# Second-half convolution taps issued among the attention's steps, and a thinner stream of modulation rows, in a two-layer mixer block

## The chip, the core and the metric

The program runs on one core of one Trainium2 chip. Its measure is device time in microseconds (us), the median of several executions. The core has five engines with their own instruction streams: TensorE (PE; its weight loads are shown apart, as PEld), VectorE (DVE), ScalarE (ACT), GpSimd (POOL) and SyncE (SP). Here PE does the matrix products, DVE and ACT the elementwise work, SP issues the loads of weight chunks, and POOL issues the loads of modulation rows.

## The reference, cut to what matters

A first block of two layers (`DEPTH = 2`), then a second block that the change doesn't touch. A layer of the first block is a mixer over 256 tokens x of width 1024 and 256 context tokens; layer 0 computes outputs for both (512 columns), layer 1 for x alone (256 columns).

```
for l in range(2):
    shift, scale, gate = split(silu(c) @ w_mod[l] + b_mod[l])      # for c and c_ctx
    h = rmsnorm(x, norm_w[l]) * (1 + scale) + shift
    p = h @ w_in[l]                                                # all branches' inputs
    r = head_norm(retention(p)) * silu(ret_z)
    s = b * conv3(c * xv) * silu(sc_z)
    f = silu(layer_norm(conv31(a * sigmoid(g)) + bias)) * silu(cf_z)
    a = windowed_attention(rope(q), rope(k), v, ctx) * silu(att_z)
    merged = sum(sigmoid(gate_i) * (branch_i @ w_branch[i]))       # r, s, f, a
    x = x + gate * (merged @ w_out[l])
# second block: its own modulation, 6 rows of columns per layer
mod = silu(c_2) @ ada_w[i] + ada_b[i]
```

`conv31` is a depthwise convolution with 31 taps over four tiles of 128 channels. Its layer norm needs all four tiles.

## The kernel before, in words

Everything is kept with channels on the partitions and tokens in the columns. Each matrix product of weights is in three parts (high and low halves in fp32r): `mm3` issues three matmuls, `tile_gemm` 24 of them for one tile of 128 outputs. A weight chunk of 512 KB is loaded by SP (`wr`), ACT makes its high half (`wh`), DVE its low half (`wl`, L169). Four chunks are held at a time. The planner of the language orders each engine's instructions: the earlier one is issued in the program, the earlier it comes, as far as its inputs are there in the planner's own clock.

The side work of a mixer (convolution, attention, layer norm, retention) stands in generators in the queue `hiq`. Each `yield` names the cost of a step in us. After every product tile the kernel calls `pump(bud)` (`proj` with `bud`, `gates` with 1.5 `bud` for each of its 8 tiles), which adds credit and issues steps from the front of `hiq` until the credit is used up. A second queue, `loq`, holds the modulation rows of the coming parts: 8 rows for layer 0's gate and 24 for layer 1 (`wmodT`), then 96 for the second block (`adaT`). One row is a 512 KB load issued by POOL (L485) into one of two buffers of the tag `ad`, and a DVE pass over it (`junk`, L495), two passes where both c and c_ctx need it. `loq` gets `ratio` times the pumped us, from the 11th pump of layer 0 and the 31st of layer 1 on.

```
self.credit = min(self.credit + us, 8.0)
while self.credit > 0 and self.hiq:
    ...
        self.credit -= next(self.hiq[0])
...
if self.pumps > 0:
    self.spare = min(self.spare + self.ratio * us, 4.0)
while self.spare > 0 and self.loq:
    c, fn = self.loq.popleft()
    self.spare -= c
    fn()
```

A row with two passes costs 2.3, with one 1.15. A pass may not come before the instruction that was issued ten marked DVE instructions earlier (`with self.tc.issue_after(self.marks[0])`; `marks` holds the last ten `tt` and `stt` instructions). `until(st, key)` issues steps from the front of `hiq`, whatever the credit, until the part named by `key` is done. `flush_lo(mark)` does the same for `loq`: at the end of layer 0 until layer 1's rows are done, at the end of layer 1 until the second block's 96 rows are done. After the latter, `ada_columns` makes `afw` from them, and each tile of the output projection of layer 1 is turned into an input of the second block with `afw` (`raw_tile`: an ACT and a DVE instruction `r<-x,afw`), for the 96 matmuls of 258 columns that follow.

The order of a mixer in product tiles: (layer 0: four tiles for the convolution's input, pumped), four query tiles, one k and one v tile; then 16 tiles of the short convolution; gates(1) (8 tiles, each 36 matmuls); `until att`; four z tiles for the attention's output; gates(3); eight q and k tiles of the retention and its v tiles (pumped 8 times with a quarter of `bud`, twice that in layer 0); `until ln`, after which `ratio` is 0.6; four z tiles, gates(2), four z tiles, gates(0); then the 8 tiles of the output projection, each pumped with 0.5.

Convolution: `conv(0)` does the taps for channel tiles 0 and 1, `conv(2)` those for tiles 2 and 3, in 31 steps each; a step is two DVE instructions (L183, `t<-t,cfw,t`). Attention: `att_prep` and the rope steps, then four `att_pair`s; 84 steps with a cost of 37.4 in layer 0, 68 steps with 25.4 in layer 1. The layer norm's steps cost 11.3 and 5.9.

Of the kernel before, what the change touches and what calls it, by code (L numbers as in the profile page):

```python
# [2 lines left out]

# [1 line left out]

# [99 lines left out]
class Core:  # L105
# [110 lines left out]
    @staticmethod  # L216
    def pipe(gens, depth):

        wait, live = deque(gens), []
        while wait or live:  # L220
            if wait and len(live) < depth:
                live.append(wait.popleft())
            for g in list(live):
                try:
                    yield next(g)
                except StopIteration:
                    live.remove(g)


    def feed(self, *src):  # L230
# [648 lines left out]
    def mixer(self, l, hs, N, first, mod, norm):  # L879
        nc, A = self.nc, self.A  # L880
        NS = N // S
        bud = (3.0, 1.0)[l]
        self.pumps, self.spare = -(10, 30)[l], 0.0
        self.ratio = (0.5, 0.6)[l]
        if l:
            self.src.extend(self.mixer_chunks(l))
        self.ahead()
# [27 lines left out]
        def conv(i):  # L915

            for j in (i, i + 1):
                us[j] = self.T(N)
                c = l * 124 + 15 * 4 + j
                self.ts(us[j], glu[j], self.cfw[:, c:c + 1], ALU.mult, self.par("cf_conv_b", l * 4 + j), ALU.add)  # L920
            yield 0.6 * NS
            for k in range(31):
                if k == 15:
                    continue
                d = k - 15
                lo, hi = max(0, -d), min(S, S - d)
                for j in (i, i + 1):
                    c = l * 124 + k * 4 + j
                    u = v3(us[j])[:, :, lo:hi]
                    self.stt(u, v3(glu[j])[:, :, lo + d:hi + d], self.cfw[:, c:c + 1], u, ALU.mult, ALU.add)  # L930
                yield 0.6 * NS
            if i == 2:
                glu.clear()
# [7 lines left out]
        def layer_norm():  # L941
            sm = self.T(N)
            self.tt(sm, us[0], us[1], ALU.add)
            self.tt(sm, sm, us[2], ALU.add)
            self.tt(sm, sm, us[3], ALU.add)
            yield 1.0 * NS
            mb = self.psa()[:, :N]
            self.mmul(mb, self.inv[512].to_broadcast([P, P]), sm)
            yield 0.1
            sq = self.T(N)  # L950
            for i in range(4):
                self.tt(us[i], us[i], mb, ALU.subtract)
                if i == 0:
                    self.act(sm, us[i], AF.Square)
                else:
                    self.act(sq, us[i], AF.Square)
                    self.tt(sm, sm, sq, ALU.add)
            yield 1.3 * NS
            rows = self.psa()[0:1, :N]
            self.row_sum(rows, 0, 1, [sm], 512, True, True)  # L960
            yield 0.1
            cols = self.columns(rows, 1, N)
            r = self.small(2 * NS)
            self.rsqrt(r, cols[:, :, 0])
            yield 0.2
            rb = self.psa()
            for t in range(2 * NS):
                self.spread(rb[:, t * P:(t + 1) * P], r[:, t:t + 1])
            yield 0.1
            for i in range(4):  # L970
                self.stt(us[i], us[i], self.par("cf_ln_w", l * 4 + i), rb[:, :N], ALU.mult, ALU.mult)
            yield 1.3 * NS
            for i in range(4):
                t = self.T(N)
                self.act(t, us[i], AF.Tanh, scale=0.5, bias=lnb2[:, i:i + 1])
                self.ts(us[i], us[i], self.par("cf_ln_b", l * 4 + i), ALU.add)
                self.stt(us[i], t, 1.0, us[i], ALU.add, ALU.mult)
                yield 0.45 * NS
            st["ln"] = 1
# [43 lines left out]
            self.hiq.append(rest())  # L1023
            self.hiq.append(conv(0))
        self.hiq.append(conv(2))
        self.hiq.append(layer_norm())


        rot, cs = const(C_ROT, 384), const(C_COS, 512)
# [28 lines left out]
        def att_prep():  # L1058
            yield from rope(kraw)
            for g in range(2):  # L1060
                pk = self.psa()
                self.mmul(pk, rot[:, P * (1 + g):P * (2 + g)], kraw)
                t = self.T()
                self.act(t, pk)
                kd.append(t)
            yield 0.1
            pv = self.psa()
            for t in range(4):
                nc.tensor.transpose(pv[:, t * P:(t + 1) * P], vraw[:, t * P:(t + 1) * P], self.ident)
            self.act(vt, pv)  # L1070
            yield 0.1
# [73 lines left out]
        def attention():  # L1145
            yield from self.pipe(gens + [att_prep()], 3)
            for t in range(4):
                yield from att_pair(t)

        self.hiq.appendleft(attention())  # L1150


        br[1] = []
# [782 lines left out]
```

## Time and profile before

| what | us |
|---|---|
| time, median of 3 runs (1773.41 to 1779.63) | 1775.39 |
| time of the profiled execution | 1777.26 |
| its span, first to last instruction | 1775.5 |
| PE busy | 1731.2 (98%) |
| DVE busy | 1360.5 (77%) |
| ACT busy | 912.4 (51%) |

A busy PE is not a PE at its peak: a matmul of the profile lasts longer than the distance to the next one's start. Where PE really stands still, a row of the timeline has the idle time in brackets, with what ended it. In the profiled execution layer 0 runs from 60 to about 720 us, layer 1 to about 1131 us.

### The profile page before, as it was taken

The numbers are of one execution on the slowest core, as the hardware profiler recorded it, in microseconds if no ns is written. First come the engines' busy times: TensorE is split into PE (matmuls) and PEld (weight loads), VectorE is DVE, ScalarE is ACT, GpSimd is POOL, SyncE is SP. The second block draws the span as 40 slices with busy tenths as digits, with TensorE's granted clock in tenths as the row PEclk, the third lists the DMA queues.
The fourth block names the chain that finished last, engine by engine and source line by source line (L and its number), as shares of the span: only waits on it lengthen the run. The fifth ranks groups of instructions, "written<-read, shape, count | busy, mean of one in ns | idle before, by whom it ended". The sixth has DMA issues, their size and how long they took to land.

```text
span 1775.5 us, 29100 instructions
## 1 busy us (share of the span) xinstructions
PE 1731.2 (98%) x11286; PEld 1543.8 (87%) x11286; DVE 1360.5 (77%) x2485; ACT 912.4 (51%) x1553; POOL 73.9 (4%) x157
## 2 busy tenths in 40 slices
PE   8999999899999999999999999999999999999998
PEld 5787788688978788898998999898999989989996
DVE  4797599966576777698499877779887669788774
ACT  5426642432342323546643555686776556656663
POOL 0000000011011110000000000100000000000000
PEclk9999999999999999999999999999999999999999
DMA  9433244467447765353476466642555633335564
GB/s 345 153 111 115 84 129 144 142 211 248 137 144 238 241 231 184 117 177 117 131 242 231 152 220 194 207 153 92 189 183 178 184 123 107 126 124 192 185 183 131
DMA packets 101883, 301.56 MB, mean 170 GB/s; under 512 B 9952, under 2 KB 21984, under 8 KB 101744
## 3 DMA queue, kind: packets, MB, share of 16 engines
q1 hardware_dynamic: 79968, 225.00, 38.9%
q0 software_dynamic: 19584, 71.31, 12.4%
q10 hardware_dynamic: 2192, 3.39, 0.6%
q8 instruction: 89, 1.46, 0.3%
q14 instruction: 50, 0.41, 0.1%
HBM read 298.61 MB, written 1.05 MB: 169 GB/s over the span
## 4 chain that ended last, share of the span: by engine, by line
PE 65%; issue 17%; DVE 7%; ACT 5%; DMA 4%; POOL 0%; SPq 0%; DVEq 0%; POOLq 0%; ACTq 0%
PE pm L186 49%; PE pa L186 13%; DMA ad<-adaT 4%; ACT t L166 3%; DVE wl L169 2%; DVE t L183 1%; DVE t L169 1%; DVE junk L495 1%; ACT wh L166 1%; PE pa L1126 1%; PE pa L551 1%; PE pa L1754 1%; PE pa L408 1%; ACT g L166 0%; PE pa L603 0%
## 5 line engine op out<-in xcount | busy, mean ns | idle before, releaser
L186 PE MATMUL pm<-r,wh 128*128 128x256 f32 (+2 forms) x4992 | 1149.5, 323 | 16.5 <-ACT r L166 9.4
L186 PEld LDWEIGHTS pm<-r,wh 128*128 128x128 f32 x4992 | 835.6, 191 | 104.5 <-ACT r L166 14.2
L186 PE MATMUL pm<-r,wl 128*128 128x256 f32 (+2 forms) x2496 | 797.5, 321 | 0.5 <-DVE wl L169 0.5
L166 ACT ACTIVATE wh<-wr 128x1024 fp32r<-128x1024 f32 (+1 forms) x406 | 425.8, 1053 | 521.3 <-PE pm L186 368.0
L169 DVE TENSOR_TENSOR wl<-wr,wh 128x1024 fp32r<-128x1024 f32 (+1 forms) x406 | 491.7, 1215 | 177.3 <-ACT wh L166 167.5
L186 PEld LDWEIGHTS pm<-r,wl 128*128 128x128 f32 x2496 | 475.2, 191 | 36.4 <-issue 1.4
L495 DVE SCALAR_TENSOR_TENSOR junk<-ad,sb_c 128x1024 bf16<-128x1024 f32 x128 | 156.1, 1219 | 59.2 <-DMA ad<-adaT 48.6
L186 PE MATMUL pa<-r,wh 128*128 128x256 f32 (+1 forms) x864 | 170.7, 295 | 5.8 <-ACT r L166 5.4
L186 PEld LDWEIGHTS pa<-r,wh 128*128 128x128 f32 x864 | 139.7, 195 | 9.5 <-ACT r L166 5.8
L169 DVE TENSOR_TENSOR t<-t,t 128x256 f32<-128x256 f32 (+2 forms) x265 | 120.7, 472 | 15.5 <-ACT t L166 13.6
L183 DVE SCALAR_TENSOR_TENSOR t<-t,cfw,t 128x482 f32<-128x482 f32 (+29 forms) x240 | 130.5, 597 | 0.0
L186 PE MATMUL pm<-wh,r 128*128 128x256 f32 (+1 forms) x560 | 127.2, 320 | 0.0
L186 PE MATMUL pa<-r,wl 128*128 128x256 f32 (+1 forms) x432 | 125.4, 294 | 0.0
L166 ACT ACTIVATE r<-t 128x256 fp32r<-128x256 f32 (+1 forms) x116 | 53.5, 470 | 108.9 <-DVE t L169 67.6
L186 PEld LDWEIGHTS pm<-wh,r 128*128 128x128 f32 x560 | 94.6, 193 | 7.3 <-issue 0.4
L186 PE MATMUL pa<-t,t 128*64 128x128 f32 (+3 forms) x668 | 89.5, 337 | 0.9 <-ACT t L166 0.8
L186 PE MATMUL pm<-wl,r 128*128 128x256 f32 (+1 forms) x280 | 89.7, 320 | 0.0
L186 PEld LDWEIGHTS pa<-r,wl 128*128 128x128 f32 x432 | 84.2, 195 | 1.3
L166 ACT ACTIVATE t<-pm 128x256 f32<-128x256 f32 (+1 forms) x172 | 78.9, 459 | 11.3 <-PE pm L186 11.2
L186 PEld LDWEIGHTS pa<-t,t 128*64 128x64 f32 (+2 forms) x668 | 66.7, 163 | 16.6 <-issue 4.5
L485 POOL DMA_DIRECT2D ad<-adaT x96 | 50.7, 529 | 636.2 <-DVE junk L495 612.4
L166 ACT ACTIVATE t<-t,s 128x512 f32<-128x512 f32 (+2 forms) x104 | 62.7, 635 | 2.9 <-DVE s L178 2.9
(217 smaller groups left out, 1313.2 us busy)
## 6 DMA issues: line engine op xcount, KB each, us to landing
wr<-win SPq DMA_DIRECT2D x172, 512.0 KB, 4.1
ad<-adaT POOLq DMA_DIRECT2D x96, 512.0 KB, 4.4
wr<-ffu SPq DMA_DIRECT2D x88, 512.0 KB, 3.6
wr<-ffd SPq DMA_DIRECT2D x38, 512.0 KB, 3.7
ad<-wmodT POOLq DMA_DIRECT2D x32, 512.0 KB, 3.8
wr<-wbr SPq DMA_DIRECT2D x32, 512.0 KB, 4.2
wr<-gli SPq DMA_DIRECT2D x24, 512.0 KB, 3.6
t<-wmodN SPq DMA_DIRECT2D x32, 256.0 KB, 5.9
```

Of the source, the lines that this page charges most:

```text
L166: return self.nc.scalar.activation(out=out, in_=in_, func=func, **k)
L169: self.marks.append(self.nc.vector.tensor_tensor(out=out, in0=a, in1=b, op=op).ins)
L183: self.marks.append(self.nc.vector.scalar_tensor_tensor(out=out, in0=a, scalar=s, in1=b, op0=op0, op1=op1).ins)
L186: self.nc.tensor.matmul(out=out, lhsT=lhsT, rhs=rhs, start=start, stop=stop)
L408: self.nc.tensor.matmul(out=rows, lhsT=lhsT, rhs=t, start=(first and i == 0), stop=(last and i == len(tiles) - 1), skip_group_check=True)
L485: self.nc.gpsimd.dma_start(out=raw, in_=self.rows.popleft())
L495: self.nc.vector.scalar_tensor_tensor(out=self.junk, in0=raw, scalar=0.5, in1=v, op0=ALU.mult, op1=ALU.mult, accum_out=o)
L551: self.nc.tensor.matmul(out=bank[:, nt * j + t:nt * j + t + 1], lhsT=q[:, t * P:(t + 1) * P], rhs=self.inv[inv], start=first and m == 0 an ...
L1126: nc.tensor.transpose(pt[:, kk * P:(kk + 1) * P], s, self.ident)
L1754: nc.tensor.matmul(out=o, lhsT=cb[:, 7 - jj:7 - jj + P], rhs=b8(hd_(X, h))[:, :, jj:8], start=(jj == 0 and h % 2 == 0), stop=(jj == 7), sk ...
```

## The change

The convolution's steps that are left when the attention is queued are no longer behind the attention but woven into it: after every third step of the attention in layer 0, and every second in layer 1, one step of the convolution is issued; what is left of it follows, and the layer norm comes last. The pump's budget goes up by a tenth. The rows' share until the layer norm is done goes down; the share after it (0.6) stays.

```
+    @staticmethod
+    def beside(main, other, n):
+        for i, cost in enumerate(main):
+            yield cost
+            if i % n == n - 1:
+                more = next(other, None)
+                if more is not None:
+                    yield more
+        yield from other
...
-        bud = (3.0, 1.0)[l]
+        bud = (3.3, 1.1)[l]
         self.pumps, self.spare = -(10, 30)[l], 0.0
-        self.ratio = (0.5, 0.6)[l]
+        self.ratio = (0.3, 0.5)[l]
...
         self.hiq.append(conv(2))
-        self.hiq.append(layer_norm())
...
-        self.hiq.appendleft(attention())
+        convs = chain(*self.hiq)
+        self.hiq = deque([self.beside(attention(), convs, (3, 2)[l]), layer_norm()])
```

No arithmetic, tile or load is added or removed.

## Rows read from the trace of the kernel before

**Rows 1.** The page's first part: busy time of each engine.

```profile
PE 1731.2 (98%) x11286; PEld 1543.8 (87%) x11286; DVE 1360.5 (77%) x2485; ACT 912.4 (51%) x1553; POOL 73.9 (4%) x157
```

**Rows 2.** Busy time by stretch: instructions (x), PE's granted clock, DMA share, GB/s.

```profile
core 0: us, PE busy (x) PEld busy (x) DVE busy (x) ACT busy (x) POOL busy (x), PEclk, DMA share, GB/s
135.00:235.00 100.00, 98.17 (x648) 78.27 (x648) 66.04 (x154) 68.66 (x156) 3.91 (x9) 1.00 0.31 99
235.00:322.00 87.00, 87.00 (x382) 71.55 (x383) 87.00 (x129) 22.98 (x28) 4.69 (x9) 1.00 0.43 142
322.00:341.00 19.00, 19.00 (x84) 14.26 (x83) 18.16 (x29) 10.71 (x16) 1.06 (x2) 1.00 0.58 190
341.00:354.00 13.00, 8.55 (x24) 5.92 (x23) 12.97 (x22) 5.32 (x9) 0.53 (x1) 0.74 0.25 81
800.00:885.00 85.00, 83.73 (x728) 77.64 (x727) 56.85 (x128) 56.89 (x113) 0.00 (x0) 1.00 0.39 124
968.00:988.00 20.00, 17.59 (x126) 16.57 (x125) 14.19 (x35) 8.09 (x13) 2.11 (x4) 0.91 0.55 178
1108.00:1131.00 23.00, 23.00 (x194) 23.00 (x193) 20.36 (x37) 17.54 (x45) 0.00 (x0) 1.00 0.58 184
```

**Rows 3.** PE's timeline, 342 to 348 us: start, duration, idle before and its end.

```profile
347.34 1.22 PE L186 MATMUL pm<-r,wh 128*128 128x512 f32 x2 [2.98 <-DVE t L183]
```

**Rows 4.** PE's timeline, 973 to 977 us.

```profile
976.52 0.67 PE L186 MATMUL pa<-t,inv 128*128 128x256 f32 x2 [2.41 <-DVE t L169]
```

**Rows 5.** DVE's groups by line, 235 to 322 us: busy, mean ns, idle before.

```profile
L183 DVE SCALAR_TENSOR_TENSOR t<-t,cfw,t 128x482 f32<-128x482 f32 (+14 forms) x60 | 40.6, 727 | 0.0
```

**Rows 6.** The tile adaT's loads up to 800 us: count, first and last start.

```profile
L485 POOL DMA_DIRECT2D ad<-adaT x69: 528/528/531, 393.2 to 705.1; - x69
```

**Rows 7.** The tile adaT's loads from 800 us on.

```profile
L485 POOL DMA_DIRECT2D ad<-adaT x27: 528/528/537, 892.3 to 1071.3; - x27
```

**Rows 8.** The tile adaT over the whole span: issue to landing.

```profile
DMA to landing us min/median/max: 3.6/4.4/7.8
```

**Rows 9.** DMA issues by line, 1048 to 1062 us: count, size, median to landing.

```profile
ad<-adaT POOLq DMA_DIRECT2D x4, 512.0 KB, 4.9
```

**Rows 10.** POOL's timeline, 412 to 443 us: three of eleven issues.

```profile
413.08 0.53 POOL L485 DMA_DIRECT2D ad<-adaT  x1 [2.95 <-DVE junk L495]
...
431.73 0.53 POOL L485 DMA_DIRECT2D ad<-adaT  x1 [3.38 <-DVE junk L495]
...
442.59 0.53 POOL L485 DMA_DIRECT2D ad<-adaT  x1 [2.36 <-DVE junk L495]
```

**Rows 11.** DVE's timeline, 429 to 433 us: the pass that frees a buffer.

```profile
430.20 1.23 DVE L495 SCALAR_TENSOR_TENSOR junk<-ad,sb_c 128x1024 bf16<-128x1024 f32 x1 [1.53 <-DMA ad<-adaT]
```

**Rows 12.** DVE's timeline, 1076 to 1150 us: the rows' end and what follows.

```profile
1084.54 1.22 DVE L495 SCALAR_TENSOR_TENSOR junk<-ad,sb_c 128x1024 bf16<-128x1024 f32 x1
...
1087.49 0.25 DVE L169 TENSOR_TENSOR ada<-ada,prm 128x96 f32<-128x96 f32 x1
...
1088.46 0.15 DVE L169 TENSOR_TENSOR afw<-cols,prm 128x8 f32<-128x8 f32 x1
...
1102.37 0.43 DVE L169 TENSOR_TENSOR r<-t,r 128x256 fp32r<-128x256 f32 x1 [0.48 <-ACT r L166]
...
1116.62 0.48 DVE L183 SCALAR_TENSOR_TENSOR r<-x,afw,r 128x256 fp32r<-128x256 f32 x1
```

**Rows 13.** ACT's timeline, 1111 to 1136 us: the first input made with afw.

```profile
1115.87 0.49 ACT L166 ACTIVATE r<-x,afw 128x256 fp32r<-128x256 f32 x1
```

**Rows 14.** PE's timeline at the end of layer 1: the first product with afw.

```profile
1130.76 0.41 PE L186 MATMUL pm<-r,wh 128*128 128x258 f32 x2
```

**Rows 15.** PE's timeline, 796 to 817 us: an attention pair's first and last products.

```profile
796.38 2.00 PE L186 MATMUL pa<-t,t 64*128 64x256 f32 x16
...
813.77 3.02 PE L186 MATMUL pa<-t,t 128*64 128x128 f32 x38
```

More of the change, by code (lines that the diff above doesn't have):

```diff
@@ L2 @@
 from contextlib import ExitStack
+from itertools import chain
 import numpy as np
```

## The prediction

> **What bounds the kernel now.** I read the page's busy times first: PE 98%, no other engine over 77% [rows 1]. So time is lost or won only where PE stands still or runs at the lower clock, and the next view is the one by stretch. In layer 0 the attention (135 to 235 us) leaves DVE a third idle; then the convolution's steps fill it wholly (235 to 322 us) without PE waiting. PE waits when the layer norm follows, between 341 and 354 us: 13.00 less 8.55 is 4.45 us idle, and the granted clock is 0.74, part of the stretch at 1.2 instead of 2.4 GHz, another 0.26 x 13 = 3.4 us [rows 2]. The timeline says for what: the first product of gates(3) that needs the attention's branch, held by DVE's L183 [rows 3], whose queue at that moment holds the norm, the modulation rows and this branch together. Layer 1 has the same place in small: 2.41 us idle between 968 and 988 us and a clock of 0.91, 1.8 us [rows 2], at the layer norm's own product, forced there by `until ln` [rows 4]. In the attention PE idles 1.83 us (layer 0) and 1.27 us (layer 1) [rows 2]. So what the change can win is bounded: 7.8 + 4.2 + 3.1 = 15.1 us.
>
> **What the change moves.** The work is the same; the order of issue follows from the credits. In layer 0 before, 10 pumps of 3.0 issue 26 of 62 convolution steps at 1.2. Attention (37.4), 36 steps (43.2) and norm (11.3) stand against 16 x 3.0 + 8 x 4.5 = 84 credits up to the end of gates(1): the norm begins at its last tile and ends in the z tiles, where rows 3 show the stall. After: 28 steps are done, 37.4 + 34 x 1.2 + 11.3 = 89.5 stand against 92.4, so the norm is issued inside gates(1). Is DVE able to follow? Moved are some 24 steps from the later stretch into the attention, at 2 x 0.68 us (40.6 us for 60 instructions) [rows 5] 33 us, and DVE has 34 us idle there [rows 2]; besides, seven rows fewer are issued by then (12 against 19, two passes each). I take the stall as gone: -7.8 us, bounds -4.5 (the clock stays low) and -7.8.
>
> In layer 1 before, 8 credits held over and 8 pumped leave 47 steps (28.2) with attention 25.4 and norm 5.9: 59.5 against 58 up to `until ln`, so the norm's end is forced. After, the attention has 34 steps of 0.6 woven in: 25.4 + 20.4 = 45.8 against 30.8 at the end of gates(1). `until att` then issues 14.4 credits at once, free of charge: the end of the third pair, the whole fourth, and 17 or so convolution steps. What is left (13.1) fits into the z tiles and gates(3), long before `until ln`. So the stall of rows 4 goes: -4.2 us, bounds -2.4 and -4.2.
>
> The forced burst is a new cost. Behind it stand the z products' evacuation and the splits that gates(3) needs. A pair takes from its first product at 796.38 to its last, starting at 813.77 and 3.02 us long, 20 us [rows 15]. PE's cover: four z tiles and the first product of gates(3), five times 23/8 = 2.9 us [rows 2], 14.4 us, and the pairs' own products, at least 5 us [rows 15]. Nearly level: bounds 0 and 8 us (a stall like that of layer 0); I take 2, nearer to nothing, because DVE had 28 us idle in this stretch before [rows 2] and the planner puts other products first where it can.
>
> In the attention itself, products now come spaced wider, but each waits behind convolution steps on DVE: between -3.1 and +5 us (four pairs in two layers, a step of 1.4 us longer in half of them); I take 0.
>
> **The rows, moved to the end.** This decides. Before, layer 0 pumps 168 credits at 0.5, 96 at 0.6 and the output tiles 4 at 0.6: 84 + 57.6 + 2.4 = 144. The 32 rows for layers 0 and 1 with their ends cost 67, the other 77 are 67 rows of `adaT` at 1.15. The trace has 69 loads by 800 us [rows 6], 67 and the two fetched ahead: the sum holds. The last 29 come in layer 1 (27 loads [rows 7]), where 30 x 0.6 + 32 x 0.6 = 37.2 pays for 32. The last pass starts at 1084.54, `afw` is there at 1088.46, used at 1115.87 [rows 12, 13]: nobody waits.
>
> After: 184.8 x 0.3 + 105.6 x 0.6 + 2.4 = 121.2 in layer 0, less 67, is 48 rows of `adaT` (the last overdraws). Layer 1 pays for 33 x 0.5 + 35.2 x 0.6 = 37.6, or 33. 96 - 48 - 33 = 15 rows are left and all issued by `flush_lo` behind gates(0). None can begin before the tenth-last marked instruction of gates(0), the split `r<-t,r` of its sixth tile, done at 1102.8 [rows 12]. From there they run through two buffers: a pass starts, 1.53 us later the next load is issued (430.20, then 431.73) [rows 10, 11], 4.4 us later it lands [rows 8]. That is 5.93 us for two rows, 2.97 each, and the fastest run of ten agrees: (442.59 - 413.08)/10 = 2.95 [rows 10]. The fifteenth pass is seven rounds after the first: 1102.8 + 41.5 = 1144.3, ends at 1145.5. From the last pass's end to `afw` I take 1.0 us, then 0.49 and 0.48 for the first `r<-x,afw` and some 0.4 between them [rows 12, 13]: PE starts the 258-column products at 1147.9 instead of 1130.76 [rows 14], 17.1 us later. The output projection, which PE does in the meantime, is the cover (23 us, rows 2) and is used up; DVE's own work queued behind the passes isn't late before that. After such a pause I add the lower clock of rows 2 (341 to 354 us), 3.4 us: 20.5 us in all.
>
> Bounds: with each landing at the fastest 3.6 us [rows 8], 7 x 5.13 ends it 5.6 us sooner and the clock costs 1.8: 13.3 us. With 4.9, as under the heavier traffic of 1048 to 1062 us [rows 9], 3.5 us later: 24 us; I stay with the median because the output projection's stretch moves only 184 GB/s of its own [rows 2].
>
> The Trainium skill, "DMA: Bandwidth & Descriptors", section "Anatomy of one DMA — SWDGE (gpsimd) path", gives 2.0 us plus bytes over 436 GB/s for a load issued by POOL. For 512 KB that is 3.2 us, an estimate from that page, against the median 4.4 here [rows 8]; by it a round is 4.7 us and the stall with the clock's 3.4 is 12.1, not 20.5. No landing of `adaT` was that quick, so the measurement decides.
>
> In layer 0's second half the rows come closer, 1.98 credits a tile against 1.8: no price, the tiles' cover is DVE's idle time there; at most 3 us if passes held up weight halves.
>
> **Sum.** 1777.26 (the profiled execution: span 1775.5 and 1.76 around it) - 7.8 - 4.2 + 2 + 0 + 20.5 = 1787.8. The median of the runs shown is 1.87 below the profiled one: **1785.9 us**, 0.6% slower. About 0.3%, 5.3 us, is what a measurement of this kernel can tell from no change.
>
> **Rivals.** (a) *The rows stay hidden, faster.* The flush costs nothing if at most 9 rows are left: (1128.4 - 1102.8 - 1.2)/2.97 + 1. That asks for six rows more by the pumps than the credits give, or for the planner to fetch them earlier; the bound of the ten marks speaks against it, for it speaks that no flush runs in this trace, so that its start is worked out and not read. Then 1775.4 - 12.0 = 1763.4, with the attention's 3 us 1760. Chance 0.18. (b) *The rows land quickly, no change.* With every landing at the fastest 3.6 us of rows 8 the stall is 13.3 and nearly equals the gains: 1775.4 - 10.0 + 13.3 = 1778.7; 12 rows left at the median landing give the same. Against it stands that only a few landings were that short. Chance 0.16. (The skill's figure above would give 1777.5.) (c) *The attention of layer 1 ends late*, at the burst's full 8 us: 1792. Speaks for it: tile buffers are shared, and the convolution's third and fourth outputs now live through the attention; against it, the cover worked out above. Chance 0.11. (d) *The norm of layer 0 stays where it was*, because DVE, 33 us fuller, lags in the attention: no -7.8, 1793.7; against it, the 34 us of idle DVE and the seven rows fewer. Chance 0.05. The forecast has 0.50; with the gains and the stall at their bounds it runs from 1775.4 - 12.0 + 13.3 = 1777 to 1775.4 - 6.9 + 2 + 24.0 = 1795.
>
> Slower is the forecast, (c) and (d): 0.66; same (b): 0.16; faster (a): 0.18. The range reaches from just above (a) to above (d): 1767 to 1797.
>
> **What would show it.** Right: no idle PE at the first products of gates(3) in layer 0 and at the norm's product in layer 1; some 50 loads of `adaT` by the end of layer 0 and some 48 passes after it, 15 of them closer than 3.2 us at the end of layer 1, past the last tile of gates(0); the 258-column products of the second block waiting for ACT's `r<-x,afw`, 15 to 20 us, and a lower clock behind that. Wrong: the last pass of `adaT` before 1128 us on this trace's clock, or a stall at layer 1's gates(3) that is larger than the one at its end.

## The result, and the profile after

| | median, us | runs | ratio to before, 95% interval |
|---|---|---|---|
| before | 1774.67 (1773.06 to 1780.81) | 6 | |
| after | 1808.54 (1803.27 to 1811.39) | 6 | 1.0184 [1.0171, 1.0198] |

The changed kernel is 1.8% slower; 1786 was forecast, 1797 the upper end. The profiled execution of after took 1803.27, the lowest of its six, so the trace below shows some 5 us less than the median has; that of before [rows 1] shows 2.6 us more than its median.

The page of after: its first part, then PE and its granted clock over 40 slices of 45 us.

```profile
span 1801.4 us, 29100 instructions
PE 1728.2 (96%) x11286; PEld 1540.6 (86%) x11286; DVE 1361.9 (76%) x2485; ACT 914.5 (51%) x1553; POOL 74.1 (4%) x157
PE   8999999999999899999999999599999999999998
PEclk9999999999999999999999999799999999999999
```

PE's busy time is 3 us less than in [rows 1] and the span 25.9 us longer: the whole loss is standing still, and one slice (1126 to 1171 us) has most of it. Where it lies by stage comes from four marks that every trace has: the span's start, layer 0's first product `pa<-r,wh` over 512 columns, and the first 258-column product of each layer's end.

| profiled execution, us | start | layer 0 | layer 1 | rest | span |
|---|---|---|---|---|---|
| before | 58.8 | 663.3 | 408.7 | 644.7 | 1775.5 |
| after | 57.1 | 663.9 | 435.2 | 645.3 | 1801.4 |

Layer 0 has gained nothing and layer 1 has lost 26.5 us. The stretches of after that answer to those of [rows 2], and new ones (PE, PEld, DVE, ACT and POOL busy, then the granted clock, DMA share, GB/s):

```profile
135.00:235.00 100.00, 96.56 (x543) 76.89 (x543) 98.74 (x195) 56.07 (x120) 4.23 (x8) 1.00 0.35 114
235.00:322.00 87.00, 86.95 (x479) 69.64 (x478) 44.43 (x76) 42.43 (x73) 1.06 (x2) 1.00 0.27 88
341.00:354.00 13.00, 13.00 (x59) 10.74 (x59) 8.86 (x12) 4.15 (x6) 0.53 (x1) 1.00 0.49 161
600.00:622.00 22.00, 16.36 (x62) 12.16 (x61) 16.85 (x24) 7.77 (x12) 2.64 (x5) 0.92 0.67 230
860.00:910.00 50.00, 43.99 (x390) 40.47 (x390) 42.30 (x99) 30.09 (x60) 1.06 (x2) 0.97 0.40 127
968.00:988.00 20.00, 20.00 (x148) 19.09 (x147) 10.21 (x19) 5.35 (x7) 0.53 (x1) 1.00 0.49 158
1108.00:1134.00 26.00, 24.40 (x200) 23.82 (x199) 21.01 (x33) 9.80 (x13) 3.70 (x7) 1.00 0.82 290
1134.00:1160.00 26.00, 4.48 (x22) 4.20 (x22) 18.30 (x38) 6.99 (x22) 3.70 (x7) 0.56 0.66 231
```

DVE now fills the attention (98.74 of 100 us) and has room behind it (44.43 of 87): the convolution has moved as worked out. Both stalls at the norm are gone; PE is busy throughout 341 to 354 us and 968 to 988 us, and layer 1's product of the norm, now at 926.81 us, waits for nothing. Three new ones stand elsewhere: 600 to 622 us, 860 to 910 us, and the 26 us before the second block. PE's timeline of after has them (idle time and its end in brackets):

```profile
605.85 0.50 PE L187 MATMUL pm<-r,wl 128*128 128x512 f32 x1 [1.52 <-DVE wl L170]
617.38 0.51 PE L187 MATMUL pm<-r,wh 128*128 128x512 f32 x1 [3.53 <-ACT r L167]
876.93 0.66 PE L1137 MATMUL pa<-ident,t 128*128 128x128 f32 x4 [1.53 <-ACT t L167]
895.16 3.74 PE L1137 MATMUL pa<-ident,t 128*128 128x128 f32 x16 [2.49 <-ACT t L167]
906.47 0.50 PE L187 MATMUL pm<-r,wh 128*128 128x256 f32 x2 [1.88 <-DVE t L184]
1156.11 1.17 PE L187 MATMUL pm<-r,wh 128*128 128x258 f32 x3 [21.52 <-ACT r L167]
```

**The long one** answers to [rows 14]. PE's row names ACT, but ACT itself stands for 16.68 us, for DVE; DVE's and ACT's timelines:

```profile
1108.74 1.22 DVE L507 SCALAR_TENSOR_TENSOR junk<-ad,sb_c 128x1024 bf16<-128x1024 f32 x1 [1.92 <-DMA ad<-adaT]
...
1148.10 1.23 DVE L507 SCALAR_TENSOR_TENSOR junk<-ad,sb_c 128x1024 bf16<-128x1024 f32 x1 [1.74 <-DMA ad<-adaT]
...
1150.40 1.23 DVE L507 SCALAR_TENSOR_TENSOR junk<-ad,sb_c 128x1024 bf16<-128x1024 f32 x1 [1.06 <-DMA ad<-adaT]
...
1153.44 1.22 DVE L507 SCALAR_TENSOR_TENSOR junk<-ad,sb_c 128x1024 bf16<-128x1024 f32 x1 [1.81 <-DMA ad<-adaT]
...
1155.35 0.16 DVE L170 TENSOR_TENSOR afw<-cols,prm 128x8 f32<-128x8 f32 x1
```

```profile
1155.00 0.21 ACT L167 ACTIVATE sh1h<-ada 128x8 fp32r<-128x8 f32 x1 [16.68 <-DVE ada L170]
...
1155.55 0.51 ACT L167 ACTIVATE r<-x,afw 128x256 fp32r<-128x256 f32 x1
```

From 1108.74 to 1153.44 us lie the last 15 passes, and each of the last ones waits for its load. So the chain is row, pass, `afw`, ACT, PE, as the prediction had it. The counts agree too: the tile `adaT` up to 800 us, in after (before: [rows 6]):

```profile
L497 POOL DMA_DIRECT2D ad<-adaT x50: 528/528/531, 512.8 to 720.3; - x50
```

**The one in layer 0** lies at the z tiles ahead of gates(0) and at gates(0)'s first product: 22.00 less 16.36 is 5.64 us idle, and 0.08 x 22 = 1.8 us of lower clock. DVE's timeline of after:

```profile
601.98 1.23 DVE L507 SCALAR_TENSOR_TENSOR junk<-ad,sb_c 128x1024 bf16<-128x1024 f32 x1 [1.11 <-DMA ad<-adaT]
603.13 0.08 DVE L507 DVE_READ_ACCUMULATOR junk<-ad,sb_c 128x1 f32 x1
603.42 1.23 DVE L507 SCALAR_TENSOR_TENSOR junk<-ad,sb_c 128x1024 bf16<-128x1024 f32 x1 [0.21 <-DMA ad<-adaT]
604.58 0.08 DVE L507 DVE_READ_ACCUMULATOR junk<-ad,sb_c 128x1 f32 x1
604.58 1.22 DVE L170 TENSOR_TENSOR wl<-wr,wh 128x1024 fp32r<-128x1024 f32 x1
```

DVE works in its written order. Two passes stand ahead of the low half `wl` of a weight chunk, whose high half ACT has ready at 601.09; both passes wait for their loads, `wl` ends at 605.80, and PE has stood for it since 604.33. At gates(0), right behind, the z tiles' splits are late in the same way (617.38).

### The profile page after: what moved, and what is told of

It is laid out like the page before. It is cut to its first block, busy times and chain, and to the rows that moved or that the text cites. A ratio compares the mean times of both kernels' runs of the same rounds, so it can differ in the third digit from the quotient of the medians.

```text
span 1801.4 us, 29100 instructions
## 1 busy us (share of the span) xinstructions
PE 1728.2 (96%) x11286; PEld 1540.6 (86%) x11286; DVE 1361.9 (76%) x2485; ACT 914.5 (51%) x1553; POOL 74.1 (4%) x157
## 3 DMA queue, kind: packets, MB, share of 16 engines
HBM read 298.61 MB, written 1.05 MB: 166 GB/s over the span
## 4 chain that ended last, share of the span: by engine, by line
PE 72%; DVE 12%; DMA 5%; issue 5%; ACT 5%; POOL 0%; DVEq 0%; SPq 0%; POOLq 0%; ACTq 0%
PE pm L187 55%; PE pa L187 14%; DMA ad<-adaT 5%; DVE t L184 3%; DVE wl L170 3%; ACT t L167 3%; DVE junk L507 2%; DVE t L170 1%; ACT wh L167 1%; DVE t L1100 1%; PE pa L563 1%; PE pa L1137 1%; PE pa L1766 1%; PE pa L420 1%; ACT g L167 0%
## 5 line engine op out<-in xcount | busy, mean ns | idle before, releaser
L184 DVE SCALAR_TENSOR_TENSOR t<-t,pm 128x256 f32<-128x256 f32 (+1 forms) x103 | 56.0, 544 | 18.2 <-ACT t L167 10.8
```

The source lines that it names most:

```text
L184: self.marks.append(self.nc.vector.scalar_tensor_tensor(out=out, in0=a, scalar=s, in1=b, op0=op0, op1=op1).ins)
```

## The experiments

My theory after the result: three separate things, namely the flush of 15 rows (by the shares), rows too close in layer 0's second half (budget 3.3 at an unchanged 0.6), and a forced burst of attention in layer 1 (the weave). The rivals: that the weave itself is what costs, whatever the rows do; and that the flush is bound not by its two buffers but by the memory's traffic. Edits are shown against after unless said otherwise; stages are those of the table above.

### Shares back

```
-        self.ratio = (0.3, 0.5)[l]
+        self.ratio = (0.5, 0.6)[l]
```

> The changed kernel with the rows' shares of before (0.5 and 0.6), all else as changed. Theory (the rows left to the end of layer 1 cost most): by the credits the last adaT row is then issued in the q and k tiles of layer 1's retention and none is left to flush; the pause of 21.7 us before the 258-column products and the lower clock behind it (about 2) go, so about 1808.5 - 24 = 1784 us, still some 10 over before. Rival (the weaving itself makes the attention late and that costs most): 1800 or more.

Measured: 1781.63, ratio 1.0037 [1.0025, 1.0049]. The pause before the second block is gone, and layer 1 takes 408.7 us where after took 435.2. So the shares, through the flush, cost 26.5 us in the traces and 26.9 in the medians (1808.54 - 1781.63); the weave and the budget are not what made the kernel 1.8% slower. Yet the order alone is still no gain: layer 0 takes 666.1.

### Shares alone

Only this, in the kernel before:

```
-        self.ratio = (0.5, 0.6)[l]
+        self.ratio = (0.3, 0.5)[l]
```

> The kernel before with nothing but the thinner shares (0.3 and 0.5). Theory: by the credits 29 rows are left to the end of layer 1; through two buffers at 5.93 us for two rows the fifteenth pair starts 83 us after 1102.8, PE's pause is about 59 us and the time about 1774.7 + 59 + 3 = 1837 us. Rival (the flush costs a fixed start and not a price for each row): about 1800. Rival (the flush is not what costs): 1775.

Measured: 1831.83, a single run, so without an interval. PE's timeline at the end of layer 1, and the loads of `adaT` from 1102 to 1180 us:

```profile
1179.92 1.17 PE L186 MATMUL pm<-r,wh 128*128 128x258 f32 x3 [59.48 <-ACT r L166]
```

```profile
L485 POOL DMA_DIRECT2D ad<-adaT x24: 528/528/537, 1102.9 to 1173.4; - x24
DMA to landing us min/median/max: 3.6/3.8/5.9
```

With some 28 rows left the pause is 59.48 us, where the ring of two buffers had given 59: the same arithmetic holds at twice the size. The last 28 passes start between 1094.68 and 1177.26 us, 3.06 us a row; only towards the end, where PE and the weight loads stand still, is a row cheaper: the median landing of the loads above is 3.8, which gives (1.53 + 3.8)/2 = 2.67 us, and the last eleven passes are 2.69 us apart. Also, layer 0 falls from 663.3 to 655.6: thinner rows remove the norm's stall by themselves, without the weave.

### A third buffer

`t2` gives up two tiles of 58 to make room.

```
-        th = self.adp.tile([P, 1024], F32, tag="ad", name=self.nm("ad"))
+        th = self.adp.tile([P, 1024], F32, tag="ad", bufs=3, name=self.nm("ad"))
...
-        for _ in range(2 - len(self.raws)):
+        for _ in range(3 - len(self.raws)):
```

> The changed kernel with three buffers for the rows in place of two (and 56 tiles in place of 58 in the mixer's pool, to make room). Theory (the flush is bound by the ring of two buffers): three loads in flight need 2.0 us a row by the landings and some 2.3 us by what the chunks leave of 400 GB/s, so 14 passes take 28 to 33 us and not 41, the pause falls from 21.7 to some 10 us, the time to about 1798 us. Rival (the passes or POOL's issue bind the flush): no change, 1808. Rival (the mixer's tiles were the bottleneck): slower than 1808.

Measured: 1794.91, ratio 1.0117 [1.0099, 1.0134], although its start takes 64.8 us (7.7 more; why was not looked into). The pause is 8.56 us in place of 21.52; the loads of `adaT` from 1100 to 1143 us:

```profile
DMA to landing us min/median/max: 4.0/5.8/7.7
```

Three loads in flight land later each (5.8 median), but more often: (1.53 + 5.8)/3 = 2.4 us a row by that sum, and the last 15 passes, from 1104.03 to 1139.71 us, are 2.55 us apart, where those of after are 3.19 apart. So the flush was bound by the ring first; the later landings show that the traffic takes part of the gain back. And layer 0 falls to 655.4: the waits of 605 and 617 us are gone, with the rows as close as in after. Product by product against after, aligned on the start of layer 0, the 8.5 us all lie between 605 and 622 us of after, so this gain is not the longer start's. The loss in layer 0, too, has to do with the rows' buffers.

### One layer at a time

Layer 0 alone: weave and `bud` 3.3 there, the rest as before.

```
-        bud = (3.3, 1.1)[l]
+        bud = (3.3, 1.0)[l]
-        self.ratio = (0.3, 0.5)[l]
+        self.ratio = (0.5, 0.6)[l]
...
+        if l == 0:
             convs = chain(*self.hiq)
             self.hiq = deque([self.beside(attention(), convs, (3, 2)[l]), layer_norm()])
+        else:
+            self.hiq.append(layer_norm())
+            self.hiq.appendleft(attention())
```

> The weaving and the higher budget in layer 0 alone, layer 1 and the first shares (0.5, 0.6) as before; after the layer norm layer 0's rows get 0.6 of 3.3 for a tile. Theory (the stall at layer 0's norm goes, 8 us, and the rows, now as close as the ring of two buffers allows, hold DVE up before gates(0), 7 us): 1774.5 us, within 3. Rival (the weave in layer 0 is a plain gain): 1767.

Measured: 1777.23, ratio 1.0018 [1.0006, 1.0029]. Layer 0 takes 666.9, no better than before, and the same two waits have returned, larger than in after (PE's timeline):

```profile
609.95 0.50 PE L187 MATMUL pm<-r,wl 128*128 128x512 f32 x1 [2.05 <-DVE wl L170]
623.13 1.52 PE L187 MATMUL pm<-r,wh 128*128 128x512 f32 x2 [4.26 <-ACT r L167]
```

Layer 1 alone: weave and `bud` 1.1 there, the rest as before (the same edit with the layers exchanged).

> The weaving and the higher budget in layer 1 alone, layer 0 and both shares as before. Theory: the wait of the layer norm in layer 1 goes (4 us), and the forced burst of the attention puts PE's waits of the changed profile between 870 and 910 us in its place (some 9 us more than before): 1774.7 + 4 = 1779 us. Rival (the weave costs nothing there): 1770. The rows end before the output projection by the credits, so no flush.

Measured: 1777.6, ratio 1.0017 [1.0007, 1.0027]; layer 1 takes 409.6 against 408.7. The norm's stall of 4.2 us is won, and spent again in the attention (PE's timeline):

```profile
876.20 0.66 PE L1137 MATMUL pa<-ident,t 128*128 128x128 f32 x4 [1.53 <-ACT t L167]
894.70 0.66 PE L1137 MATMUL pa<-ident,t 128*128 128x128 f32 x4 [2.77 <-ACT t L167]
905.23 0.50 PE L187 MATMUL pm<-r,wh 128*128 128x256 f32 x2 [1.76 <-DVE t L184]
```

### Layer 0 with the old distance of its rows

To the kernel of layer 0 alone, one number: 3.3 x 0.545 is 1.8 credits a tile again.

```
-        self.ratio = (0.6, 0.6)[l]
+        self.ratio = (0.545, 0.6)[l]
```

> The same as the kernel with layer 0 alone, but with 0.545 in place of 0.6 for layer 0's rows after the norm, so that a tile pays for 1.8 as before. Theory (the waits of PE near 605 to 617 us come from the rows' rate): they go, 1768 us, some 7 below the kernel with layer 0 alone. Rival (they come from the weaving or the order): no difference between the two.

Measured: 1766.7, ratio 0.9957 [0.9941, 0.9972]. It beats both kernels. Layer 0 takes 657.4, 9.5 us less than with 0.6. The stretch from 520 to 720 us, in after, in layer 0 alone with 0.6, in this one, and with the third buffer:

```profile
520.00:720.00 200.00, 194.37 (x847) 159.56 (x846) 145.09 (x213) 61.86 (x96) 24.84 (x47) 0.99 0.64 215
```

```profile
520.00:720.00 200.00, 193.69 (x837) 159.12 (x836) 145.44 (x213) 61.59 (x93) 25.48 (x48) 0.97 0.64 218
```

```profile
520.00:720.00 200.00, 199.14 (x897) 165.16 (x896) 143.71 (x210) 64.14 (x101) 23.36 (x44) 1.00 0.63 213
```

```profile
520.00:720.00 200.00, 200.00 (x892) 165.72 (x891) 152.47 (x224) 67.11 (x101) 25.84 (x49) 1.00 0.66 221
```

PE's idle time and lower clock go with fewer row loads in the stretch (POOL's count, 48 against 44) or with a third buffer; the weave is in all four.

### Is the weave needed?

Without it, both budgets raised, with the rows' distance kept:

```
-        self.ratio = (0.3, 0.5)[l]
+        self.ratio = (0.5, 0.6)[l]
...
-        convs = chain(*self.hiq)
-        self.hiq = deque([self.beside(attention(), convs, (3, 2)[l]), layer_norm()])
+        self.hiq.append(layer_norm())
+        self.hiq.appendleft(attention())
...
-        self.ratio = (0.6, 0.6)[l]
+        self.ratio = (0.545, 0.545)[l]
```

> No weaving: the order of before in both layers, with the budget up by a tenth, the first shares 0.5 and 0.6, and 0.545 after the norm in both. By the credits the norm of layer 0 is issued inside gates(1) and that of layer 1 in the retention's q and k tiles, as with the weave. Theory A (what moves the norms early is the budget): both stalls go, 1774.5 - 7.8 - 4.2 = 1762.5 us. Theory B (DVE must also be filled in the attention, so layer 0's stall needs the weave): only layer 1's goes, 1770 us, or DVE lags further and it is 1775.

Measured: 1781.02, ratio 1.0035 [1.0023, 1.0048]; both forecasts missed. Layer 0 takes 661.9: the norm is issued sooner, but PE waits for it directly (PE's timeline):

```profile
317.69 0.73 PE L187 MATMUL pm<-r,wh 128*128 128x512 f32 x2 [2.52 <-ACT t L167]
```

Layer 1 takes 412.1. Next, the same with the weave in layer 0 (`if l == 0`, as above):

> The weave in layer 0 alone, the budget up by a tenth in both layers, the first shares 0.5 and 0.6, and 0.545 after the norm. Theory A: the same 1762.5 us as without any weave. Theory B: layer 0's stall goes with the weave and layer 1's by the budget, 1762.5 us, and the kernel without a weave is some 8 us slower than this one.

Measured: 1773.96, ratio 0.9999 [0.9986, 1.0011]. In layer 0 the weave is worth 7.1 us by the medians (in the traces 655.9 in place of 661.9), when the rows before the norm are not thinned. But every theory had this kernel at 1762.5: layer 1 takes 411.7 where it took 404.1 with `bud` 1.0 and 0.6 behind the norm. Two waits for ACT's `t` are there (PE's timeline). Budget and share behind the norm were changed together in layer 1; which of them brings the waits was not tried.

```profile
934.24 0.51 PE L187 MATMUL pm<-r,wh 128*128 128x256 f32 x2 [1.71 <-ACT t L167]
962.00 0.72 PE L187 MATMUL pm<-r,wh 128*128 128x512 f32 x2 [2.43 <-ACT t L167]
```

### The whole change, with the rows kept

After, with the old shares and 0.545 behind the norm in layer 0:

```
-        self.ratio = (0.3, 0.5)[l]
+        self.ratio = (0.5, 0.6)[l]
...
-        self.ratio = (0.6, 0.6)[l]
+        self.ratio = (0.545, 0.6)[l]
```

> The weave and the budget of the changed kernel in both layers, with the rows' shares of before: 0.5 and 0.6 until the norm, 0.545 and 0.6 after it, so that a tile of layer 0 pays for 1.8 as before. Theory (the weave itself gains 6 to 8 us in layer 0 and nothing in layer 1, where the norm's wait is traded for the attention's; all the rest was the rows): 1781.6 of the kernel with the first shares back, less the 9 us of the rows before gates(0), 1772 us, some 5 above the kernel with layer 0 alone. Rival (the weave of layer 1 costs once the rows are out of the way): 1777 or more. Rival (it gains there too): 1767 or less.

Measured: 1773.55, ratio 0.9995 [0.9985, 1.0006]: no change. Against the shares put back alone, layer 0 falls from 666.1 to 656.2, the second pair of runs in which 0.545 is worth 9 to 10 us in the traces (by the medians 8.1 us here and 10.5 in the first pair). Against the best kernel, layer 1 takes 410.7 in place of 404.1. The stretch of its attention's end in this one and in the best:

```profile
855.00:905.00 50.00, 43.72 (x380) 40.35 (x377) 43.10 (x102) 29.81 (x60) 2.09 (x4) 0.97 0.42 138
```

```profile
855.00:905.00 50.00, 50.00 (x424) 48.72 (x425) 33.61 (x59) 29.09 (x51) 1.59 (x3) 1.00 0.55 180
```

With layer 1's weave and budget PE stands for 6.28 us there; without them it never does. The two were not separated in this place.

## Why the prediction was right in its sign and too low

**Layer 0's norm, -7.8: right.** What [rows 3] shows has no counterpart in after. Product by product against before, aligned on the start of layer 0, after is 1.0 us behind at 331.52 us (the attention, taken at 0), 5.7 ahead at 343.99 and 6.5 ahead at 517.01. With the rows' distance kept, layer 0 as a whole gives back 663.3 - 656.2 = 7.1. Two changes act here, and either is enough: the weave with the rows not thinned (the last kernel above), and the thinner rows without a weave.

**Layer 1's norm, -4.2: the number right, its cause not.** The prediction had the stall from the credits, with the norm forced by `until ln`. But 4.1 to 4.6 us go already when layer 0 alone is changed (layer 1 takes 404.6 and 404.1 in place of 408.7), although layer 1's code, budget and shares are then those of before. DVE's timeline of before, just ahead of the product of [rows 4]:

```profile
974.80 1.23 DVE L495 SCALAR_TENSOR_TENSOR junk<-ad,sb_c 128x1024 bf16<-128x1024 f32 x1 [2.19 <-DMA ad<-adaT]
...
975.95 0.42 DVE L169 TENSOR_TENSOR t<-t,t 128x256 f32<-128x256 f32 x1
```

and the same place in the best kernel, DVE and PE:

```profile
964.39 1.22 DVE L507 SCALAR_TENSOR_TENSOR junk<-ad,sb_c 128x1024 bf16<-128x1024 f32 x1
...
965.53 0.43 DVE L170 TENSOR_TENSOR t<-t,t 128x256 f32<-128x256 f32 x1
```

```profile
966.10 0.67 PE L187 MATMUL pa<-t,inv 128*128 128x256 f32 x2
```

A row's pass stands ahead of the norm's `t` in both. In before it waits 2.19 us for its load, in the other its load is there, and PE's wait falls from 2.41 to 0.12 us. So this stall was a row's load too, and that the change removed it by issuing the norm sooner was in part luck: rows that arrive at another moment do it as well. (A slip in the same paragraph: 45.8 - 30.8 is 15.0 and not 14.4; nothing hangs on it.)

**Rows closer in layer 0's second half, "no price, [...] at most 3 us": the step that failed.** In after itself layer 0 goes from 6.5 us ahead of before at 517 us to 0.5 behind at its end, a loss of 7.0 us, nearly all of it between 605 and 622 us. With 0.6 against 0.545 it measured 9.5 and 9.9 us in the two pairs, and 8.5 by the third buffer (663.9 - 655.4). It eats the whole gain of layer 0. The working had the numbers. Three products of 512 columns start every 0.68 us, a tile of 24 so takes 5.4 us, and 1.98/1.15 = 1.72 rows in a tile are one every 3.2 us, against 2.97 for the ring at the median landing. Before, it was one every 3.5 us. At 3.2 a landing of 5 us (the longest of layer 0's 50 took 7.1) puts a pass late, and DVE, in its order, holds `wl` and the splits behind it. The prediction had named this way, passes that hold up weight halves, and priced it too low. "The tiles' cover is DVE's idle time" was wrong, because most of that idle time is the wait: in 520 to 720 us DVE is idle for some 54 us before, and waits for these loads for 33.8 us of it, 34.6 in after, 31.6 in the best kernel and 7.4 with three buffers (the view of the tile `junk`: its engine's idle time before it). The sum hardly differs; what differs is how much DVE must do beside it. In the 80 us ahead of the product that waits at 605.85 us, 23 to 24 passes stand in the three kernels with two buffers and 1.98 credits (DVE waits 23 to 25 us for their loads), and 21 to 22 in before and the two with 1.8 (18 to 22 us). So in the first three DVE ends this `wl` just as PE starts on it, having kept PE waiting, and in the others 0.9 to 3.8 us ahead of PE; with three buffers it is 25 passes, 7.7 us of waiting, and 3.6 us ahead.

**The flush, +20.5: the mechanism right, the size low.** Fifteen rows, 50 loads in layer 0, two buffers, the 258-column products waiting through ACT: all there. The cost is 26.5. The pause is 21.5 in place of 17.1: the first of the 15 passes starts at 1108.74, not 1102.8, and the last at 1153.44, 44.7 us later, not 41.5. Aligned on the start of layer 1, product by product, PE is 2.5 us behind the kernel with the shares put back when the output projection starts, and 5.0 at its end (26.5 - 21.5), with waits like the 1.05 us for ACT's `r` at 1115.29 in between.

**The lower clock behind the pause, +3.4: there, and made up elsewhere.** From 1156 to 1160 us it is 0.50, the 1.2 GHz level, after PE has stood for 21.52 us; the first 24 products behind the pause take 5.3 us, where they take 2.9 in the kernel with the shares put back, and none of them but the first waits. Some 20 us later both kernels have a wait of 3.2 us for ACT's `r`. Behind it the clock of after stays up and the other's falls, which gives back 1.5 us at once; at the span's end 0.4 is left. The stretches of after (the first two) and of the kernel with the shares put back:

```profile
1156.00:1160.00 4.00, 3.89 (x17) 3.81 (x18) 3.90 (x10) 4.00 (x18) 0.00 (x0) 0.50 0.00 0
1176.00:1181.00 5.00, 4.64 (x36) 4.52 (x36) 4.84 (x12) 1.70 (x4) 0.00 (x0) 1.00 0.89 351
```

```profile
1151.00:1156.00 5.00, 4.82 (x27) 4.82 (x28) 4.84 (x13) 1.65 (x4) 0.00 (x0) 0.66 0.94 329
```

So 645.3 us for the rest of the span against 644.9 doesn't show that the pause is free behind its end. Behind the pause of 59.48 us the rest takes 650.1, behind that of 8.56 us 647.9, and without a pause 644.1 to 646.7 in eight traces.

**The landings.** The 13 loads of after from 1108 us on have a median of 4.3, near the 4.4 that I took from [rows 8]; with the shares alone it falls to 3.8, where little else is loaded. The Trainium skill, "DMA: Bandwidth & Descriptors", section "Anatomy of one DMA — SWDGE (gpsimd) path", has 2.0 us plus bytes over 436 GB/s, an estimate of 3.2 us for 512 KB; the shortest load of `adaT` in these runs took 3.6 us, so the measurement decides, and the more so with three in flight (5.8).

**Layer 1's burst, +2: too low, towards rival (c).** It measured 6.6 (410.7 - 404.1), or 5.1 in layer 1 alone (409.6 - 408.7 + 4.2), of its bounds of 0 to 8; both figures hold the higher budget too. So layer 1 without the flush comes out at 0 to +2 (408.7, 409.6 and 410.7 against 408.7) and not at -2.2. The cover that I had counted assumed that PE can do z tiles during the burst; the waits at 876.93 and 895.16 are inside it, at the transposes. Ahead of the first of them DVE's timeline (871.81 to 875.14 us) has woven convolution steps and one row's pass between the attention's own steps, which delays what ACT needs.

The sum again, with what was measured: 1774.7 - 6.5 + 7.0 (layer 0) - 4.6 + 6.6 (layer 1) + 26.9 = 1804.1, against 1808.5. About 4 us are left without a name; my terms come from single traces, and a stage whose code is the same takes up to 3 us more in one trace than in another (the rest: 644.1 to 646.7 without a pause).

## What to carry to other kernels

A side stream through a ring of buffers has a rate of its own, (pass to next issue + landing) / buffers: set the stream's pace clearly below it, and compare the two before you call a closer pace free (here 2.97 us by that sum, 3.19 measured in the flush of after, against a pace of 3.2 that cost and one of 3.5 that did not). An engine's idle time that ends with "waits for a load" is not free capacity when that engine issues in a fixed order; everything written behind the wait pays for it. When a stall names an engine, look at what stood ahead in that engine's order: layer 1's norm seemed late, and it was a load. When a share of a credit is changed, add up what remains at the deadline: here 15 rows at 1.8 us each (26.9/15) undid more than all that the new order could win, while the weave and budget in layer 0 alone, with its rows' pace kept, are 0.4% faster (4.6 us of it in layer 1, by the rows' other timing there).

## What the runs showed of the hardware

A 512 KB load issued by POOL lands later, the more of them are in flight: 4.3 us median with two and 5.8 with three, both beside weight loads; with two and little beside them it was 3.8. The third buffer still brought a row each 2.55 us in place of 3.19. And behind a pause of 21.5 us PE ran at 0.50 of its clock, which cost 2.4 us within 24 products although none of them but the first waited; where PE stood for 3.2 us some 20 us later, the clock fell behind it in one kernel (0.66 over 5 us) and not in the other (1.00).
